# Score products of a sparse-attention branch: keys stacked as high and low rows, low queries beside rows of zeros

## The chip, the core and the metric

The kernel runs on one core of a Trainium2 chip. Its engines are named as in the profile: PE (TensorE, matrix products; PEld is its loading of stationary operands), DVE (VectorE), ACT (ScalarE), POOL (GpSimd) and SP (SyncE, which issues most DMAs). The metric is the device time of one execution in microseconds (us); the number given for a kernel is the median of its runs.

## What is computed

One layer of a hybrid decoder with 256 tokens and a width of 2048. One wide projection of x feeds four branches (spatial gating, a gated recurrence, sparse attention, attention into memory tokens); each branch is gated, projected to 2048 columns and merged, and an output projection with a residual and a LayerNorm closes the layer. The change lies in the sparse attention. With 256 tokens its "selected" and "window" branches both see every key up to the query, so both are ordinary causal attention with their own keys and values; four key/value heads serve 16 query heads of 64 columns:

```python
s = jnp.einsum('bhgqd,bhqnkd->bhgqnk', q_b, ks).astype(f32).reshape(...) + bias
p = masked_softmax(s, mask)
o_s = jnp.einsum('bhgqnk,bhqnkd->bhgqd', p.astype(vs.dtype), vs)
...
s_w = jnp.einsum('bhgqd,bhkd->bhgqk', q_b, kw).astype(f32) + bias_w
p_w = masked_softmax(s_w, mask_w)
o_w = jnp.einsum('bhgqk,bhkd->bhgqd', p_w.astype(vw.dtype), vw)
...
o = g[0] * o_c + g[1] * o_s + g[2] * o_w
```

## The kernel before

Everything is float32. A large product is made from operands that are split in two parts of the type fp32r: the high part is a cast (ACT), the low part is what the cast left over (DVE). Of the four part products three are taken: high by high, high by low, low by high. The weights (some 240 MB) come from HBM in chunks of 1024 words on each of 128 partitions. `prepare` (lines 161 to 184) loads a chunk, casts it (`whi`) and subtracts (`wlo`), two chunks ahead of its use; three buffers hold the high parts and three the low parts. Two loops use the chunks: `gemm_b` (lines 191 to 209) keeps the weights in PE and moves 256 tokens, high and low side by side, past them (lines 202 and 203, tile `mmb`); `gemm_a` (lines 218 to 232) keeps the tokens and moves 512 weight columns past them, three products for each of two token tiles (lines 214 to 216, tile `mma`).

All other work is cut into items, closures that are put into a list by `start_side(items, chunks)`. After each chunk of a large product `pump` runs as many items as `len(items) / chunks` says, so the number of items and the number of chunks set at which chunk an item comes. What an item does on ACT and DVE is put behind the newest split of weights. The order of the instructions on each engine is then fixed ahead of the run by a scheduler that works with its own estimate of times. Engines take their instructions strictly in this order.

The two lists of items that matter here:

- The first runs beside the value projections of the two branches (lines 499 to 517, tile `vs`, 12 chunks of up to 840 words). Its items are four times `make_flat` (lines 418 to 428: four DVE additions into `flat`, a cast and a subtraction into `fhl`) and four times `split_k` (lines 489 to 497). `split_k` makes, for a pair of key heads, the high part of each head's 64 key rows on both halves of the partitions (`khd`, two casts for each head) and the low part in place (`klo`, one subtraction for each head).
- The second runs beside the merge of the memory branch and the projection after it, 48 chunks (lines 657 to 665). For each pair of query heads j, `split_q` (lines 592 to 599) puts the high part of a head's queries on its own 64 partitions and the low part on the other 64; `nsa_probs` (lines 601 to 629) makes the scores of one head, 512 keys for the second 128 queries (`s1`) and 256 for the first 128 (`s0`), and the softmax; `nsa_trans` transposes the probabilities (lines 635 to 637, tile `pt`); `nsa_values` (lines 642 to 654, tile `po`) multiplies them with the values, in products with 64 output rows (line 651).

A head's scores take four products: line 608 has 128 rows (high and low queries, against the high keys on both halves), line 609 has 64 rows (high queries against the low keys), and lines 611 and 612 do the same for the first 128 queries. The profile names the score tiles `s`.

Of the kernel before, what the change touches and what calls it, by code (L numbers as in the profile page):

```python
# [14 lines left out]
P = 128  # L15
# [3 lines left out]
CH = 1024            # float32 words of one weight chunk on a partition (512 KB in all)  # L19
# [3 lines left out]
NWV = 280            # columns of the chunks that hold values and gate logits  # L23

# [1 line left out]
BUCKET_COUNTS = [1] * 16 + [5, 6, 8, 11, 13, 18, 22, 29, 38, 50, 40]  # L26

# [7 lines left out]
NB = 16 * P // CH          # chunks of one 128-column product  # L35
NA = 16 * 512 // CH        # chunks of one 512-column product over 2048 rows
NH = 8 * 512 // CH         # the same over 1024 rows
# [12 lines left out]
def tile_hybrid_layer(ctx: ExitStack, tc: tile.TileContext, wb, wv, xT, memT, x, params, cmpp, biasp, consts,  # L50
# [19 lines left out]
    # ================= helpers =================  # L70
# [27 lines left out]
    def after(later, earlier):  # L98
        """both on one engine: later is issued after earlier."""
        tc.add_manual_dep(later.ins, earlier.ins.name,  # L100
                          mybir.DependencyInfo(mybir.DependencyClass.NoSync, mybir.DependencyReason.DATA),
                          reason="order on the engine")

# [1 line left out]
    # An item's work on VectorE and ScalarE is issued after the newest split of weights before it.  # L105
# [85 lines left out]
    def gemm_b(src, d, evac=None):  # L191
        """[128 columns, 256 tokens] into d: the weights stay, both parts of the tokens move past them at once."""
        ps = psum(mm, "mmb")
        nk = CH // P
        for c in range(NB):
            hi, lo = next_chunk()
            for kk in range(nk):
                k = c * nk + kk
                xs = src[k // 8][:, k % 8]
                wh = hi[:, kk * P:(kk + 1) * P]  # L200
                wl = lo[:, kk * P:(kk + 1) * P]
                nc.tensor.matmul(ps, wh, xs, start=(k == 0), stop=False)  # L202
                nc.tensor.matmul(ps[:, 256:512], wl, xs[:, 0:256], start=False, stop=(k == 15))  # L203
            if c == NB - 1:
                vec.tensor_copy(d, ps[:, 0:256])
                vec.tensor_add(d, d, ps[:, 256:512])
                if evac:
                    evac()
            pump()
# [8 lines left out]
    def gemm_a(src, nkt, evac):  # L218
        """[128 tokens, 512 columns] for both token tiles: the tokens stay, the weights move."""
# [14 lines left out]
    def rstd(y, v, name, w=1, follow=None):  # L234
        """y = 1 / sqrt(v + eps), with one Newton step."""
# [15 lines left out]
    # ================= memory values and keys =================  # L251
    def load_hl(src, hl, i, part=None):
        """k tiles 2 i and 2 i + 1 of the tokens, split."""
# [61 lines left out]
    # ================= memory attention =================  # L315
# [11 lines left out]
    def o_store(hl, j, o_ps, g):  # L327
        """o * silu gate, split into the two parts of the operand."""
        o = prob("oraw", 256)
        vec.tensor_mul(o, o_ps, g)  # L330
        split(hl[:, j, 0:256], hl[:, j, 256:512], o)
# [4 lines left out]
    def mm_3(ps, w, c0, xs, first, last):  # L336
        """columns c0.. of w (high parts in front, low parts 256 behind) with 256 moving columns."""
# [53 lines left out]
    # ================= projections of the sparse attention =================  # L391
    # in the order k_c, v_c, k_s, k_w; two key/value head pairs each
# [19 lines left out]
    # its two parts side by side: one product of both with the high part of w1, one of the high part with the low one  # L412
# [73 lines left out]
    khd = [big("kh0", "khd0", F32R, (P, 2, 512)), big("kh1", "khd1", F32R, (P, 2, 512))]  # L486
    klo = big("va1", "klo", F32R, (P, 2, 512))

    def split_k(pr, br):
        src = kbr[br][pr]  # L490
        cs = slice(br * 256, (br + 1) * 256)
        for half in range(2):
            hs = slice(half * 64, half * 64 + 64)
            os = slice(64 - half * 64, 128 - half * 64)
            act.copy(khd[half][hs, pr, cs], src[hs])
            act.copy(khd[half][os, pr, cs], src[hs])
            vec.tensor_sub(klo[hs, pr, cs], src[hs], khd[half][hs, pr, cs].bitcast(F32))

    start_side([lambda b=b, pr=pr: make_flat(b, pr) for b in range(2) for pr in range(2)] +
               [lambda pr=pr, br=br: split_k(pr, br) for br in range(2) for pr in range(2)], 11)  # L500

# [90 lines left out]
    def split_q(j):  # L592
        q = scr("qs", 512, F32R).rearrange("p (h t) -> p h t", h=2)
        for half in range(2):
# [3 lines left out]
            vec.tensor_sub(q[os, half], qT[j][hs], q[hs, half].bitcast(F32))  # L598
        qs[j] = q

    def nsa_probs(j, half):
        hs = slice(half * 64, half * 64 + 64)
        hd = 2 * j + half
        q = qs[j]
        kh, kl = khd[half][:, j // 4], klo[:, j // 4]
        s1 = psum(scp, "s1")
        s0 = psum(scp, "s0")
        nc.tensor.matmul(s1, q[:, half, P:256], kh, start=True, stop=False)
        nc.tensor.matmul(s1, q[hs, half, P:256], kl[hs], start=False, stop=True)  # L609
        k0 = lambda a: a.rearrange("p (b k) -> p b k", b=2)[:, :, 0:P]  # L610
        nc.tensor.matmul(s0[:, 0:256], q[:, half, 0:P], k0(kh), start=True, stop=False)
        nc.tensor.matmul(s0[:, 0:256], q[hs, half, 0:P], k0(kl[hs]), start=False, stop=True)
# [54 lines left out]
    # ================= merge of the branches =================  # L667
# [26 lines left out]
    # ================= convolution and RG-LRU =================  # L694
    # softplus(-lambda) = max(-lambda, 0) + log1p(exp(-|lambda|)), log1p(u) = 2 atanh(u / (2 + u))
# [54 lines left out]
    def lru_tanh():  # L750
        # t = tanh(-log_a / 2) = (1 - a) / (1 + a): 1 - a = 2 t / (1 + t), 1 - a^2 = 4 t / (1 + t)^2
# [20 lines left out]
    def lru_scan(c):  # L772
        t, s = ri[:, c, 0:256], ri[:, c, 256:512]
        w, v = lqs[c][:, 0:256], lqs[c][:, 256:512]
        # w = 1 / (s (1 + t)); one Newton step of the root: 2 sqrt(t) = s + t / s
# [21 lines left out]
    # ================= chunked spatial gating =================  # L797
# [111 lines left out]
    # ================= output projection, residual, norm =================  # L909
# [60 lines left out]
def _chunks_b(w, c0, n):  # L970
    """n column tiles of 128: [128 rows of a k tile, k tiles, 128]."""
# [9 lines left out]
def _chunks_a(w, c0, width=512):  # L981
    """one column tile of 512: [128 rows of a k tile, k tiles, 512]."""
# [94 lines left out]
```

## Time and profile before

| what | value |
|---|---|
| time, median of 3 runs | 1308.05 us (1307.18 to 1309.77) |
| the profiled execution: span from first to last instruction | 1305.8 us |
| PE busy | 1279.2 us (98%) |
| DVE busy | 836.7 us (64%) |
| ACT busy | 654.0 us (50%) |
| POOL busy | 122.7 us (9%) |
| mean granted clock of PE | 0.993 of full speed |
| chain that ended last | PE 89%, POOL 5%, DVE 3%, DMA 2%, ACT 1% |

The span is the profiled execution's own time between its first and its last instruction; the measured time of a run also holds what lies around it, here 1308.05 - 1305.8 = 2.25 us by the median. Busy time of PE is modelled: products overlap, so one of them shows as some 390 ns in the list of instructions even where the next ends 230 ns later. What a product costs in a gapless stretch is its step in the chain of waits, the time from the end of the one before to its own end.

### The profile page before, as it was taken

How to read it: one execution, taken by the hardware profiler on the slowest of the kernel's cores; microseconds unless marked ns; L12 is line 12 of the kernel's file. 1: busy time of each engine (PE TensorE's matmuls, PEld its weight loads, DVE VectorE, ACT ScalarE, POOL GpSimd, SP SyncE). 2: the span in 40 equal slices, each digit the busy share in tenths (PEclk: the TensorE clock that was granted, in tenths of full speed). 3: DMA queues.
4: the chain of work that ended last, by engine and by line, in shares of the span. 5: the costliest groups of instructions: out<-in, count | busy, mean ns of one | idle time of the engine just before them, and what ended most of it. 6: DMA issues, size and time to landing. Idle time of an engine off the chain costs nothing.

```text
span 1305.8 us, 17559 instructions
## 1 busy us (share of the span) xinstructions
PE 1279.2 (98%) x6588; PEld 1070.8 (82%) x6588; DVE 836.7 (64%) x1306; ACT 654.0 (50%) x921; POOL 122.7 (9%) x128
## 2 busy tenths in 40 slices
PE   8999999999999999999999899999999999999996
PEld 6888898988887777778888688888888888888886
DVE  6666665686557566677667896455556555555556
ACT  6544564375448656655763454444444444444442
POOL 0000000000000000002289800000000000000001
PEclk9999999999999999999999899999999999999998
DMA  9766659567565444446555566666666666668662
GB/s 314 239 191 181 179 150 206 159 214 237 180 190 162 146 138 137 146 130 193 167 172 178 154 209 201 188 192 194 195 199 192 195 193 195 184 187 320 191 214 79
DMA packets 74699, 244.57 MB, mean 187 GB/s; under 512 B 8663, under 2 KB 14967, under 8 KB 74103
## 3 DMA queue, kind: packets, MB, share of 16 engines
q1 hardware_dynamic: 70752, 235.53, 59.3%
q10 hardware_dynamic: 3863, 7.93, 2.6%
q8 instruction: 51, 0.84, 0.3%
q14 instruction: 33, 0.27, 0.1%
HBM read 240.94 MB, written 2.49 MB: 186 GB/s over the span
## 4 chain that ended last, share of the span: by engine, by line
PE 89%; POOL 5%; DVE 3%; DMA 2%; ACT 1%; issue 1%; SPq 0%; ACTq 0%
PE mmb L202 19%; PE mma L215 17%; PE mma L214 17%; PE mma L216 17%; PE mmb L203 10%; DMA raw<-in_wb 2%; DVE wlo L114 1%; PE po L651 1%; POOL ri L764 1%; POOL lq L766 1%; DVE flat L114 1%; PE mmd L216 1%; PE mmd L215 1%; PE mmd L214 1%; PE s L609 1%
## 5 line engine op out<-in xcount | busy, mean ns | idle before, releaser
L114 DVE TENSOR_TENSOR wlo<-raw,whi 128x1024 fp32r<-128x1024 f32 (+2 forms) x429 | 529.2, 1235 | 384.3 <-ACT whi L114 377.2
L114 ACT CAST whi<-raw 128x1024 fp32r<-128x1024 f32 (+2 forms) x429 | 446.7, 1042 | 514.1 <-PE mma L216 277.6
L202 PE MATMUL mmb<-xhl,whi 128*128 128x512 f32 x1152 | 411.4, 400 | 5.9 <-ACT whi L114 5.9
L203 PE MATMUL mmb<-xhl,wlo 128*128 128x256 f32 x1152 | 325.6, 283 | 2.5 <-DVE wlo L114 2.5
L202 PEld LDWEIGHTS mmb<-xhl,whi 128*128 128x128 f32 x1152 | 217.7, 189 | 57.5 <-ACT whi L114 6.9
L215 PE MATMUL mma<-wlo,xhl 128*128 128x512 f32 x576 | 226.4, 393 | 0.0
L203 PEld LDWEIGHTS mmb<-xhl,wlo 128*128 128x128 f32 x1152 | 219.0, 190 | 7.3 <-DVE wlo L114 5.0
L216 PE MATMUL mma<-whi,xhl 128*128 128x512 f32 x576 | 224.8, 390 | 0.0
L214 PE MATMUL mma<-whi,xhl 128*128 128x512 f32 x576 | 206.9, 392 | 0.0
L215 PEld LDWEIGHTS mma<-wlo,xhl 128*128 128x128 f32 x576 | 108.2, 188 | 21.9 <-issue 0.6
L216 PEld LDWEIGHTS mma<-whi,xhl 128*128 128x128 f32 x576 | 108.2, 188 | 21.9
L214 PEld LDWEIGHTS mma<-whi,xhl 128*128 128x128 f32 x576 | 107.7, 188 | 22.4 <-issue 0.4
L736 POOL CAST lwhl<-lw 128x256 fp32r<-128x256 f32 x8 | 5.9, 744 | 622.9 <-DVE oc L114 605.2
L202 PE MATMUL mmb<-memhl,whi 128*128 128x512 f32 x128 | 45.3, 399 | 0.0
L114 ACT ACT_TABLE_LOAD x31 | 39.8, 1283 | 3.8 <-issue 1.6
L215 PE MATMUL mma<-wlo,mT 128*128 128x512 f32 x96 | 37.5, 390 | 0.0
L216 PE MATMUL mma<-whi,mT 128*128 128x512 f32 x96 | 37.4, 390 | 0.0
L203 PE MATMUL mmb<-memhl,wlo 128*128 128x256 f32 x128 | 35.9, 281 | 0.0
L214 PE MATMUL mma<-whi,mT 128*128 128x512 f32 x96 | 33.6, 390 | 0.0
L114 ACT ACTIVATE p<-p,mn 128x256 f32<-128x256 f32 x64 | 28.6, 448 | 7.3 <-DVE mn L114 5.4
L875 POOL TENSOR_TENSOR ws<-ws,smask 128x128 f32<-128x128 f32 x8 | 6.7, 840 | 269.9 <-DMA ws<-in_sguw 269.9
L202 PEld LDWEIGHTS mmb<-memhl,whi 128*128 128x128 f32 x128 | 24.1, 188 | 6.0
(301 smaller groups left out, 1677.7 us busy)
## 6 DMA issues: line engine op xcount, KB each, us to landing
raw<-in_wb SPq DMA_DIRECT2D x423, 512.0 KB, 4.2
raw<-in_wv SPq DMA_DIRECT2D x10, 420.0 KB, 3.3
traw<-in_xT SPq DMA_DIRECT2D x8, 256.0 KB, 5.8
bt<-bdr ACTq DMA_DIRECT2D x8, 256.0 KB, 11.2
z<-in_x ACTq DMA_DIRECT2D x1, 2048.0 KB, 9.2
out<-z SPq DMA_DIRECT2D x8, 256.0 KB, 2.3
traw<-in_memT SPq DMA_DIRECT2D x7, 256.0 KB, 6.0
lw<-in_lruw SPq DMA_DIRECT2D x8, 128.0 KB, 4.4
```

The lines of the kernel that those rows point to most:

```text
L114: ins = getattr(getattr(nc, self.name), op)(*a, **k)
L202: nc.tensor.matmul(ps, wh, xs, start=(k == 0), stop=False)
L203: nc.tensor.matmul(ps[:, 256:512], wl, xs[:, 0:256], start=False, stop=(k == 15))
L214: nc.tensor.matmul(ps, xh, wh, start=first, stop=False)
L215: nc.tensor.matmul(ps, xh, wl, start=False, stop=False)
L216: nc.tensor.matmul(ps, xl, wh, start=False, stop=last)
L609: nc.tensor.matmul(s1, q[hs, half, P:256], kl[hs], start=False, stop=True)
L651: nc.tensor.matmul(po[hs, kt * P:256], vsw[:, kt, br, kvh * 64:(kvh + 1) * 64], pT[:, 256:384] if kt else pT[:, 0:256], start=False, stop= ...
L736: nc.gpsimd.tensor_copy(lws[c][:, 0:256], lw)
L764: nc.gpsimd.tensor_scalar(s, s, 2.0 ** -55, 1e-30, op0=ALU.mult, op1=ALU.max)
L766: nc.gpsimd.tensor_mul(w, v, s)
L875: nc.gpsimd.tensor_mul(ws[:, 0:P], ws[:, 0:P], smask)
```

## The change

The key tiles `khd` become `khl`: a head's high rows stay on its own half, and its low rows stand on the other half. The tile `klo` goes; its place takes `qlz`, which holds the low queries of a head on its own half and zeros on the other, for two pairs of heads in turn. The tile of high queries `q` now has the high part on both halves. Each of the four products of a head has 128 rows: high queries (twice) against high and low keys, and low queries over zeros against the same. The products keep their number and their numbers of columns. A new item `zero_rows` with two memsets makes the list of 8 items a list of 9, over the same 11 chunks. All else in the two files differs only in comments.

```diff
-    khd = [big("kh0", "khd0", F32R, (P, 2, 512)), big("kh1", "khd1", F32R, (P, 2, 512))]
-    klo = big("va1", "klo", F32R, (P, 2, 512))
+    khl = [big("kh0", "khl0", F32R, (P, 2, 512)), big("kh1", "khl1", F32R, (P, 2, 512))]
+
+    qlz = big("va1", "qlz", F32R, (P, 2, 2, 256))
...
-            act.copy(khd[half][hs, pr, cs], src[hs])
-            act.copy(khd[half][os, pr, cs], src[hs])
-            vec.tensor_sub(klo[hs, pr, cs], src[hs], khd[half][hs, pr, cs].bitcast(F32))
+            act.copy(khl[half][hs, pr, cs], src[hs])
+            vec.tensor_sub(khl[half][os, pr, cs], src[hs], khl[half][hs, pr, cs].bitcast(F32))
+
+    def zero_rows():
+        for half in range(2):
+            vec.memset(qlz[64 - half * 64:128 - half * 64, :, half].bitcast(F32), 0.0)
 
     start_side([lambda b=b, pr=pr: make_flat(b, pr) for b in range(2) for pr in range(2)] +
-               [lambda pr=pr, br=br: split_k(pr, br) for br in range(2) for pr in range(2)], 11)
+               [lambda pr=pr, br=br: split_k(pr, br) for br in range(2) for pr in range(2)] + [zero_rows], 11)
...
             act.copy(q[hs, half], qT[j][hs])
-            vec.tensor_sub(q[os, half], qT[j][hs], q[hs, half].bitcast(F32))
+            act.copy(q[os, half], qT[j][hs])
+            vec.tensor_sub(qlz[hs, j % 2, half], qT[j][hs], q[hs, half].bitcast(F32))
...
-        kh, kl = khd[half][:, j // 4], klo[:, j // 4]
+        k1 = khl[half][:, j // 4]
+        k0 = k1.rearrange("p (b k) -> p b k", b=2)[:, :, 0:P]
         s1 = psum(scp, "s1")
         s0 = psum(scp, "s0")
-        nc.tensor.matmul(s1, q[:, half, P:256], kh, start=True, stop=False)
-        nc.tensor.matmul(s1, q[hs, half, P:256], kl[hs], start=False, stop=True)
-        k0 = lambda a: a.rearrange("p (b k) -> p b k", b=2)[:, :, 0:P]
-        nc.tensor.matmul(s0[:, 0:256], q[:, half, 0:P], k0(kh), start=True, stop=False)
-        nc.tensor.matmul(s0[:, 0:256], q[hs, half, 0:P], k0(kl[hs]), start=False, stop=True)
+
+        nc.tensor.matmul(s1, q[:, half, P:256], k1, start=True, stop=False)
+        nc.tensor.matmul(s1, qlz[:, j % 2, half, P:256], k1, start=False, stop=True)
+        nc.tensor.matmul(s0[:, 0:256], q[:, half, 0:P], k0, start=True, stop=False)
+        nc.tensor.matmul(s0[:, 0:256], qlz[:, j % 2, half, 0:P], k0, start=False, stop=True)
```

The scheduler's order changes with it. Three places are shown; the names are tiles, with a number where several tiles share a name, and the score products stand on lines 614 to 617 of the changed kernel, the value products on line 656.

PE, one head's scores in the merge of the memory branch, before:

```order
L216 MATMUL mma_3847<-whi,om 128x512
L608 MATMUL s_3896<-khd_2328,qs 128x512
L609 MATMUL s_3896<-klo,qs 128x512
L611 MATMUL s_3897<-khd_2328,qs 128x256
L612 MATMUL s_3897<-klo,qs 128x256
L214 MATMUL mma_3846<-whi,om 128x512
```

and in the changed kernel:

```order
L216 MATMUL mma_3843<-whi,om 128x512
L614 MATMUL s_3892<-khl_2328,qs 128x512
L615 MATMUL s_3892<-khl_2328,qlz 128x512
L616 MATMUL s_3893<-khl_2328,qs 128x256
L617 MATMUL s_3893<-khl_2328,qlz 128x256
L214 MATMUL mma_3842<-whi,om 128x512
```

The four products stand in the same place; only their operands differ.

DVE, beside the value projections, from the last chunk of the first branch on, before (`raw` numbers are weight chunks, `gate` the logits behind the first branch):

```order
L114 TENSOR_TENSOR wlo<-raw_2417,whi 128x280
L114 TENSOR_TENSOR fhl<-flat,fhl 128x16x30
L114 TENSOR_TENSOR wlo<-raw_2441,whi 128x840
L114 TENSOR_TENSOR flat<-kv_2023,cpar 64x16x15 x4
L114 TENSOR_TENSOR wlo<-raw_2471,whi 128x840
L114 TENSOR_TENSOR flat<-kv_2071,cpar 64x16x15 x4
L114 TENSOR_TENSOR gate<-vs_2331,gb 128x24
L114 TENSOR_TENSOR gate<-vs_2332,gb 128x24
L114 TENSOR_TENSOR wlo<-raw_2495,whi 128x840
```

and in the changed kernel:

```order
L114 TENSOR_TENSOR wlo<-raw_2417,whi 128x280
L114 TENSOR_TENSOR flat<-kv_2023,cpar 64x16x15 x4
L114 TENSOR_TENSOR fhl<-flat,fhl 128x16x30
L114 TENSOR_TENSOR wlo<-raw_2447,whi 128x840
L114 TENSOR_TENSOR flat<-kv_2071,cpar 64x16x15 x4
L114 TENSOR_TENSOR fhl<-flat,fhl 128x16x30
L114 TENSOR_TENSOR wlo<-raw_2477,whi 128x840
L114 TENSOR_TENSOR gate<-vs_2331,gb 128x24
L114 TENSOR_TENSOR gate<-vs_2332,gb 128x24
L114 TENSOR_TENSOR wlo<-raw_2495,whi 128x840
```

The third and the fourth group of `flat` additions each stand one chunk earlier, ahead of a `wlo` that they stood behind.

PE, the value products of the second pair of heads, before:

```order
L644 MATMUL po<-pcT_3754,vbd 128x256
L651 MATMUL po<-pT,vsw 64x128 x2
L651 MATMUL po<-pT,vsw 64x256 x2
L651 MATMUL po<-pT,vsw 64x128 x2
L651 MATMUL po<-pT,vsw 64x256 x2
L215 MATMUL mma_4321<-wlo,om 128x512
```

and in the changed kernel:

```order
L649 MATMUL po<-pcT_3748,vbd 128x256
L656 MATMUL po<-pT,vsw 64x128 x2
L656 MATMUL po<-pT,vsw 64x256 x2
L656 MATMUL po<-pT,vsw 64x128
L216 MATMUL mma_4321<-whi,om 128x512
L214 MATMUL mma_4320<-whi,om 128x512
L215 MATMUL mma_4320<-wlo,om 128x512
L216 MATMUL mma_4320<-whi,om 128x512
L214 MATMUL mma_4321<-whi,om 128x512
L656 MATMUL po<-pT,vsw 64x128
L656 MATMUL po<-pT,vsw 64x256 x2
L215 MATMUL mma_4321<-wlo,om 128x512
```

Here one run of eight products with 64 output rows became two runs with five large products between them. Over all eight pairs there were 12 such runs before and there are 13 now.

## Rows read from the trace of the kernel before

**Rows 1.** First lines of the page: span, then busy us, share, instructions.

```profile
span 1305.8 us, 17559 instructions
PE 1279.2 (98%) x6588; PEld 1070.8 (82%) x6588; DVE 836.7 (64%) x1306; ACT 654.0 (50%) x921; POOL 122.7 (9%) x128
```

**Rows 2.** Stretch: us, busy PE, PEld, DVE, ACT, POOL, PE clock, DMA.

```profile
395.00:610.00 215.00, 215.00 (x1078) 166.16 (x1077) 147.64 (x434) 135.77 (x274) 4.37 (x6) 1.00 0.49 147
```

**Rows 3.** Chain of waits, one head's scores: start us, us, what.

```profile
461.76 0.23 PE s L608
461.99 0.42 PE s L609
462.41 0.32 PE s L611
462.73 0.31 PE s L612
463.04 0.43 PE mma L214
```

**Rows 4.** Chain of waits, transposes behind another head's scores.

```profile
427.88 0.26 PE pt L635
428.14 0.11 PE pt L636
```

**Rows 5.** Chain of waits, the one L611 that stands behind transposes.

```profile
529.09 0.12 PE s L611
```

**Rows 6.** Chain of waits, a 256-column product near the end.

```profile
1272.40 0.12 PE mmd L214
```

**Rows 7.** Stationary loads of line 608: ns min/median/max, first and last us, form.

```profile
L608 PEld LDWEIGHTS s<-khd,qs x16: 186/187/189, 402.0 to 579.8; 128*128 128x128 f32 x16
```

**Rows 8.** DVE in order of time: start us, us, instruction, count.

```profile
261.08 0.65 DVE L114 TENSOR_TENSOR fhl<-flat,fhl 128x480 fp32r<-128x480 f32 x1
261.65 1.02 DVE L114 TENSOR_TENSOR wlo<-raw,whi 128x840 fp32r<-128x840 f32 x1
262.60 2.34 DVE L114 TENSOR_TENSOR flat<-kv,cpar 64x240 f32<-64x240 f32 x4
264.97 1.03 DVE L114 TENSOR_TENSOR wlo<-raw,whi 128x840 fp32r<-128x840 f32 x1
265.92 2.34 DVE L114 TENSOR_TENSOR flat<-kv,cpar 64x240 f32<-64x240 f32 x4
```

**Rows 9.** PE there, first low product of three chunks; in brackets the wait.

```profile
266.06 0.40 PE L215 MATMUL vs<-wlo,xhl 128*128 128x280 f32 x1 [0.75 <-DVE wlo L114]
...
274.40 0.29 PE L215 MATMUL vs<-wlo,xhl 128*128 128x280 f32 x1
...
276.71 0.29 PE L215 MATMUL vs<-wlo,xhl 128*128 128x280 f32 x1
```

**Rows 10.** Chain of waits, value products of one pair in two runs.

```profile
478.33 1.01 PE po L651 x10
...
480.24 0.79 PE po L651 x5
```

**Rows 11.** Chain of waits, value products of another pair, unbroken.

```profile
502.36 1.45 PE po L651 x16
```

**Rows 12.** Groups by line and shape, ACT: count, busy us, mean ns, idle.

```profile
L114 ACT CAST qs<-q 64x256 fp32r<-64x256 f32 x16 | 6.4, 402 | 0.2
```

**Rows 13.** Groups by line and shape, DVE: memsets of 512 words.

```profile
L114 DVE MEMSET pc<- 128x512 f32 x2 | 1.0, 485 | 0.1
```

**Rows 14.** DVE, the low part of one chunk in the score stage.

```profile
411.62 1.23 DVE L114 TENSOR_TENSOR wlo<-raw,whi 128x1024 fp32r<-128x1024 f32 x1
```

**Rows 15.** PE, its first product with that low part.

```profile
415.06 0.40 PE L215 MATMUL mma<-wlo,om 128*128 128x512 f32 x1
```

**Rows 16.** ACT, held until POOL releases a buffer.

```profile
722.10 1.04 ACT L114 CAST whi<-raw 128x1024 fp32r<-128x1024 f32 x1 [9.82 <-POOL ri L783]
```

**Rows 17.** PE behind that cast.

```profile
723.20 0.80 PE L202 MATMUL mmb<-xhl,whi 128*128 128x512 f32 x1 [5.04 <-ACT whi L114]
```

More of the change, by code (lines that the diff above doesn't have):

```diff
@@ L597, in split_q @@
             act.copy(q[hs, half], qT[j][hs])
-            vec.tensor_sub(q[os, half], qT[j][hs], q[hs, half].bitcast(F32))
+            act.copy(q[os, half], qT[j][hs])
+            vec.tensor_sub(qlz[hs, j % 2, half], qT[j][hs], q[hs, half].bitcast(F32))
         qs[j] = q
     def nsa_probs(j, half):
-        hs = slice(half * 64, half * 64 + 64)
         hd = 2 * j + half
         q = qs[j]
-        kh, kl = khd[half][:, j // 4], klo[:, j // 4]
+        k1 = khl[half][:, j // 4]
+        k0 = k1.rearrange("p (b k) -> p b k", b=2)[:, :, 0:P]
         s1 = psum(scp, "s1")
         s0 = psum(scp, "s0")
-        nc.tensor.matmul(s1, q[:, half, P:256], kh, start=True, stop=False)
-        nc.tensor.matmul(s1, q[hs, half, P:256], kl[hs], start=False, stop=True)
-        k0 = lambda a: a.rearrange("p (b k) -> p b k", b=2)[:, :, 0:P]
-        nc.tensor.matmul(s0[:, 0:256], q[:, half, 0:P], k0(kh), start=True, stop=False)
-        nc.tensor.matmul(s0[:, 0:256], q[hs, half, 0:P], k0(kl[hs]), start=False, stop=True)
+        nc.tensor.matmul(s1, q[:, half, P:256], k1, start=True, stop=False)
+        nc.tensor.matmul(s1, qlz[:, j % 2, half, P:256], k1, start=False, stop=True)
+        nc.tensor.matmul(s0[:, 0:256], q[:, half, 0:P], k0, start=True, stop=False)
+        nc.tensor.matmul(s0[:, 0:256], qlz[:, j % 2, half, 0:P], k0, start=False, stop=True)
         for br in range(2):
```

## Prediction

> **What bounds the kernel now.** I read the head of the page first. PE is busy for 1279.2 of 1305.8 us [rows 1], so a gain must come out of PE's own sequence, and a loss shows as a wait of PE. Then I looked at the stage that holds the score products, the stretch from 395 to 610 us: PE is busy in all of its 215.00 us at a clock of 1.00, that is 2.4 GHz, while DVE works for 147.64 and ACT for 135.77 us [rows 2]. PE waits for nobody there, so every step that leaves PE's chain in this stretch moves the end by its own length, as long as ACT and DVE keep up.
>
> Next came the chain of waits at one head's scores, where the reader compares steps of equal column counts [rows 3]. Line 608, with 128 rows and 512 columns, takes 0.23 us. Line 609, also 512 columns but 64 rows, takes 0.42. Lines 611 and 612 have 256 columns each and take 0.32 and 0.31, and the large product behind them, which takes 0.23 elsewhere, takes 0.43. A transpose behind the scores takes 0.26 where the next takes 0.11 [rows 4]. So some 0.2 us is added at each passage from 128 rows to 64 and from 64 to 128. It belongs to the passage and not to the line: the one line 611 that follows transposes with 128 rows takes 0.12 [rows 5]. The size agrees with a stationary load of 187 ns that is no longer hidden [rows 7].
>
> **The change: the score products.** Nothing is removed from PE but these passages. The new steps are taken from products with 128 rows: 0.23 for 512 columns [rows 3] and 0.12 for 256 columns, each with a stationary operand of its own [rows 5, 6]. A head followed by a large product costs 0.42 + 0.32 + 0.31 + 0.43 = 1.48 us with its follower now, and 0.23 + 0.12 + 0.12 + 0.23 = 0.70 then: 0.78 saved. A head followed by a transpose goes from 1.31 (0.26 in place of 0.43) to 0.58: 0.73 saved. The chain shows 7 heads of the first kind, 8 of the second, and one that is broken by transposes and loses four passages as well (0.74). The sum is 7 x 0.78 + 8 x 0.73 + 0.74 = 12.0 us. The value products with 64 output rows keep their own passages.
>
> The row just read also weighs a rule. Line 608 uses all 128 rows, follows a product that does so too, and still takes 0.23 us with a load of 187 ns [rows 3, 7]: that load lay beside the product before it. The Trainium skill says otherwise (TensorE: Matmul & The Clock Gate, The mechanism): a load of weights overlaps products in flight only when their row groups differ. By that rule the new products would hide no load at all, and the gain would be none; the trace speaks against it here. This is rival 1 below.
>
> **The change: the list of nine items.** Nine items in place of eight over the same 11 chunks come at chunks 2, 3, 4, 5, 7 and on in place of 2, 3, 5, 6, 7, 9 and on. The third and fourth group of `flat` additions thereby stand ahead of a `wlo` that they stood behind, and DVE is what PE waits for just there [rows 9]. Worked forward in DVE's order with the steps of before: the first `fhl` starts at 261.08, and the four additions take 2.34 [rows 8], so they end at 263.42, `fhl` (261.65 - 261.08 = 0.57) at 263.99, and `wlo` 1.03 later at 265.02 against 262.67. From its next start at 264.94 (a step is 262.60 - 261.65 = 0.95) four additions, `fhl` and `wlo` follow: 264.94 + 2.34 + 0.57 + 1.03 = 268.88, against 266.00 now. PE's first low product of this chunk then starts at 268.94 in place of 266.06, 2.9 us late. Part of that is made good, since the following `wlo` has now no `flat` group before it: it ends some 1.2 us later, at 270.0, before PE needs it. PE goes on at its pace of 276.71 - 274.40 = 2.31 us a chunk [rows 9]. Four chunks on it stands at 268.94 + 4 x 2.31 = 278.18, against 276.71: 1.5 us late. The bounds are 0 (the weights of these chunks come late for another reason in both kernels) and 2.9 (nothing is made good). I take 1.5, the value of the worked order.
>
> The two memsets write 512 words on 64 partitions each. A memset of 512 words on 128 partitions takes 485 ns [rows 13], so they add 1.0 us to DVE behind the last of the eight old items, where by the count above PE's need lies over 1 us later. I count 0; without that cover it is 1.0.
>
> **The change: value products.** The new order has 13 runs of products with 64 output rows in place of 12. A pair in two runs costs 1.01 + 0.79 us [rows 10] plus one more large product at 0.43 in place of 0.23; an unbroken pair costs 1.45 [rows 11]. The difference is 0.55 us, lost. Bounds are 0 and 1.1.
>
> **The change: casts.** Eight casts of 64 rows leave ACT at 264 to 277 us, where ACT waits anyway: nothing gained. In the score stage 16 casts of 0.402 us are added [rows 12], 6.4 us on an ACT with 79 us to spare [rows 2]. Behind each pair of them stands the `whi` of a coming chunk, and behind that its `wlo` and PE. The tightest chunk that I found has its low part at 411.62 + 1.23 = 412.85 [rows 14] and is first used at 415.06 [rows 15]: 2.2 us of cover against 0.8 us of casts and at most two heads' gain (1.5 us). It is just enough, and elsewhere the cover is 2.5 us or more. I count 0; bounds 0 and 6.4. DVE's subtractions only change their target. No DMA is added; on SP one load for the recurrence changes places with one weight chunk in this stage, where PE has no wait to lengthen.
>
> **A wait further on.** At 712 to 722 us ACT is held for 9.82 us by a DMA that it has to issue into a buffer that POOL still uses [rows 16], and PE waits 5.04 us for the cast behind it [rows 17]. The change swaps some of POOL's instructions in this recurrence, with the same instructions ahead of the one that frees the buffer. PE, ACT and POOL all arrive earlier together, so I count 0; bounds are -5.0 (the wait goes) and +5.0 (it doubles).
>
> **The sum.** -12.0 + 1.5 + 0.55 = -10.0 us. Against the profiled execution: 1305.8 - 10.0 = 1295.8 us of span, and with the 2.25 us around it, which the change doesn't touch, 1298.1 us, which is also 10.0 below the median of 1308.05.
>
> **Rivals.**
> 1. *The loads stay in the open.* If a load can't be hidden between two products that use the same rows, then the first score product, the three behind it and the follower each pay 0.2 us: five passages a head in place of four, 16 x 0.2 = 3.2 us more than now, with 1.5 and 0.55 lost besides: 1313.3 us, slower. It decides at the step of the second product of a head: 0.4 us rather than 0.23. For it speaks only that these operands come from new tiles; against it that 0.23 and 0.12 are paid everywhere else with 128 rows [rows 3, 6].
> 2. *ACT comes late.* The added casts push `whi` behind PE's need, and PE waits for all 6.4 us: 1304.5 us. For it speaks the cover of 2.2 us in the first heads, against it that ACT stands idle for a third of the stage [rows 2].
> 3. *The wait behind POOL changes size.* POOL's new order frees the buffer earlier or later and moves PE's 5.04 us by its whole length: 1293.1 or 1303.1 us.
>
> **How the numbers follow.** The forecast has a chance of 0.74, with 1294.5 to 1302 as its own range from the bounds of 1.5, 0.55 and part of the last term. Rival 1 has 0.04, rival 2 0.10, rival 3 0.12 with both signs. The range of 1293.0 to 1303.2 us takes in the forecast and rival 3, 0.86 in all. A difference of 0.2% (2.6 us) is about what the measurement can tell from no change. Faster by more holds the forecast, rival 3 and most of rival 2: 0.92. Within 0.2%: 0.04. Slower: 0.04.
>
> **What would show it.** In the chain of the changed kernel lines 614 to 617 should step by 0.23, 0.23, 0.12 and 0.12 us and the follower by 0.23 or 0.11; a 0.4 there is rival 1. PE's waits for `wlo` at 262 to 271 us should grow from under 2 us to about 3.2. There should be no wait of PE for `whi` or `wlo` between 395 and 600 us; several are rival 2. The wait behind POOL near 712 us (ten earlier than now) should stay near 5 us. A time above 1305 us would mean that the passages were not what costs 0.2 us, or that their gain is given back at a place that I hold for covered.

## The result and the profile after

The changed kernel takes 1298.51 us (median), against 1308.05 before: a ratio of 0.9924, with an interval of 0.9911 to 0.9936. The forecast was 1298.1. The profiled execution of that timing was disturbed and took 3658 us, so the profile shown here is from a second timing of the same kernel (1298.62 us, ratio 0.9921, interval 0.9904 to 0.9938; its profiled execution 1298.26 us).

The head of its page, in the columns of [rows 1]:

```profile
span 1296.1 us, 17572 instructions
PE 1268.3 (98%) x6588; PEld 1071.4 (83%) x6588; DVE 836.9 (65%) x1308; ACT 655.8 (51%) x929; POOL 124.8 (10%) x128
```

PE executes as many instructions as before and is busy 10.9 us less; the span is 9.7 us shorter. So the gain lies in PE's own sequence, and 1.2 us of it went into further waits. The stretch of the score products, as in [rows 2]:

```profile
395.00:610.00 215.00, 215.00 (x1136) 175.35 (x1135) 155.67 (x447) 148.87 (x303) 8.60 (x10) 1.00 0.52 158
```

PE is still busy throughout at a clock of 1.00 (2.4 GHz), and gets 1136 instructions done where it did 1078. ACT now works for 148.87 us of the 215.

A head's scores in the chain of waits (start us, us, what), which answers to [rows 3, 4]; lines 614 to 617 are the four products, 640 is the transpose behind them:

```profile
426.35 0.23 PE s L614
426.58 0.23 PE s L615
426.80 0.12 PE s L616
426.92 0.12 PE s L617
427.04 0.11 PE pt L640
```

The stationary loads of the second of these lines, grouped as in [rows 7]:

```profile
L615 PEld LDWEIGHTS s<-khl,qlz x16: 187/188/192, 403.3 to 572.1; 128*128 128x128 f32 x16
```

The steps are 0.23, 0.23, 0.12 and 0.12 us, and the transpose takes 0.11 in place of 0.26: no product pays for a passage. The loads of 187 to 192 ns lie beside products that use the same 128 rows. Here the rule that stood behind rival 1 (the Trainium skill, TensorE: Matmul & The Clock Gate, The mechanism: a load overlaps products in flight only where the row groups differ) is contradicted by the trace. The same section also lets a load into a background weight buffer go ahead of products in flight, and that would fit.

PE's waits by releaser (total us, times, longest):

```profile
PE mmb L202 <- ACT whi L114: 7.7, 2, 6.6
PE vs L215 <- DVE wlo L114: 3.5, 2, 2.3
```

The second line is the list of nine items; the first is the wait behind POOL. Both in order of time (start us, us, instruction, in brackets the wait and its releaser): PE at the values, as in [rows 9], then ACT and PE behind POOL, as in [rows 16, 17]:

```profile
264.69 0.40 PE L215 MATMUL vs<-wlo,xhl 128*128 128x280 f32 x1 [2.25 <-DVE wlo L114]
...
268.56 0.40 PE L215 MATMUL vs<-wlo,xhl 128*128 128x280 f32 x1 [1.27 <-DVE wlo L114]
```

```profile
712.57 1.99 ACT L114 CAST whi<-raw 128x1024 fp32r<-128x1024 f32 x2 [11.42 <-POOL ri L788]
```

```profile
713.67 0.79 PE L202 MATMUL mmb<-xhl,whi 128*128 128x512 f32 x1 [6.64 <-ACT whi L114]
```

Four landmarks cut the span into pieces: the first and last high product of the values (`vs`, line 216), ACT's last Gelu of `vact`, and the first product of the last merge (`mT`, line 214). The end of the scores lies between the second and the third. For before and after in that order (min/median/max ns, first to last start):

```profile
L216 PE MATMUL vs<-whi,xhl x64: 287/291/298, 250.3 to 277.1; 128*128 128x280 f32 x64
L114 ACT ACTIVATE vact<-mma x4: 590/597/600, 636.2 to 664.0; 128x512 f32<-128x512 f32 x4
L214 PE MATMUL mma<-whi,mT x96: 389/389/476, 1204.2 to 1271.1; 128*128 128x512 f32 x96
```

```profile
L216 PE MATMUL vs<-whi,xhl x64: 287/291/293, 249.9 to 278.3; 128*128 128x280 f32 x64
L114 ACT ACTIVATE vact<-mma x4: 592/595/599, 626.4 to 653.6; 128x512 f32<-128x512 f32 x4
L214 PE MATMUL mma<-whi,mT x96: 389/389/476, 1194.5 to 1261.4; 128*128 128x512 f32 x96
```

| stretch | before | after | difference | forecast |
|---|---|---|---|---|
| start to first `vs` | 250.3 | 249.9 | -0.4 | 0 |
| first to last `vs` | 26.8 | 28.4 | +1.6 | +1.5 |
| last `vs` to last `vact` | 386.9 | 375.3 | -11.6 | -12.0 + 0.55 |
| last `vact` to first `mT` | 540.2 | 540.9 | +0.7 | 0 (-5 to +5) |
| first `mT` to the end | 101.6 | 101.6 | 0.0 | 0 |

### The profile page after: what moved, and what is told of

It is laid out like the page before. It is cut to its first block, busy times and chain, and to the rows that moved or that the text cites. A ratio compares the mean times of both kernels' runs of the same rounds, so it can differ in the third digit from the quotient of the medians.

```text
span 3656.6 us, 17572 instructions
## 1 busy us (share of the span) xinstructions
PE 3643.2 (100%) x6588; PEld 2353.9 (64%) x6588; DVE 831.4 (23%) x1308; ACT 662.8 (18%) x929; POOL 99.1 (3%) x128
## 4 chain that ended last, share of the span: by engine, by line
PE 100%; DVE 0%; ACT 0%; ACTq 0%; issue 0%
PE mmb L202 26%; PE mma L215 17%; PE mma L214 17%; PE mma L216 17%; PE mmb L203 13%; PE po L656 1%; PE vs L214 1%; PE vs L216 1%; PE vs L215 1%; PE mmd L215 1%; PE mmd L216 1%; PE mmd L214 1%; PE hps L442 0%; PE hps L441 0%; PE pt L641 0%; PE s L615 0%
## 5 line engine op out<-in xcount | busy, mean ns | idle before, releaser
L202 PE MATMUL mmb<-xhl,whi 128*128 128x512 f32 x1152 | 1123.0, 978 | 0.0
L203 PE MATMUL mmb<-xhl,wlo 128*128 128x256 f32 x1152 | 707.3, 614 | 0.0
L202 PEld LDWEIGHTS mmb<-xhl,whi 128*128 128x128 f32 x1152 | 452.4, 393 | 344.9 <-issue 342.0
L215 PE MATMUL mma<-wlo,xhl 128*128 128x512 f32 x576 | 494.7, 859 | 0.0
L216 PE MATMUL mma<-whi,xhl 128*128 128x512 f32 x576 | 490.5, 852 | 0.0
L203 PEld LDWEIGHTS mmb<-xhl,wlo 128*128 128x128 f32 x1152 | 470.0, 408 | 25.8 <-issue 7.1
L214 PE MATMUL mma<-whi,xhl 128*128 128x512 f32 x576 | 465.4, 854 | 0.0
L214 PEld LDWEIGHTS mma<-whi,xhl 128*128 128x128 f32 x576 | 206.8, 360 | 142.4 <-issue 140.6
L215 PEld LDWEIGHTS mma<-wlo,xhl 128*128 128x128 f32 x576 | 207.1, 360 | 141.0 <-issue 139.3
L216 PEld LDWEIGHTS mma<-whi,xhl 128*128 128x128 f32 x576 | 207.6, 360 | 140.0 <-issue 139.6
L202 PE MATMUL mmb<-memhl,whi 128*128 128x512 f32 x128 | 140.6, 1098 | 0.0
L216 PE MATMUL mma<-whi,memhl 128*128 128x512 f32 x64 | 69.6, 1097 | 0.0
L214 PE MATMUL mma<-whi,memhl 128*128 128x512 f32 x64 | 66.0, 1101 | 0.0
```

Source lines behind the costliest of these rows:

```text
L214: nc.tensor.matmul(ps, xh, wh, start=first, stop=False)
L215: nc.tensor.matmul(ps, xh, wl, start=False, stop=False)
L216: nc.tensor.matmul(ps, xl, wh, start=False, stop=last)
```

## The experiments

Every kernel was timed beside the kernel before on the same chip, in four sets; its time there was 1309.12 us (e1 to e4), 1309.29 (e5 to e8), 1308.52 (e9 to e11) and 1309.37 (e12). Ratios are against that. "The score stretch" below is the third line of the table.

**e1: the changed kernel again.**

> The changed kernel once more, for an undisturbed trace. By the prediction's steps: lines 614 to 617 step by 0.23, 0.23, 0.12, 0.12 us, the follower by 0.23 or 0.11; PE waits about 3.2 us for wlo beside the value projections (1.7 before); no wait between 395 and 600 us; the wait behind POOL near 5 us. Time 1298.5 us. If instead ACT came late or the gain came from elsewhere, waits appear in the score stage, or the steps of 615 and 617 stay at 0.4 and 0.3 us and the time was won at another place.

1298.62 us, and all steps as above. It is the base for what follows.

**e2: eight items again, the memsets inside the last of them.**

```diff
     def split_k(pr, br):
+        if pr and br:
+            zero_rows()
...
-               [... for br in range(2) for pr in range(2)] + [zero_rows], 11)
+               [... for br in range(2) for pr in range(2)], 11)
```

> The changed kernel with the two memsets inside the last of the eight old items, so that the list has 8 items over 11 chunks as before. If the nine-item list costs what was worked out, PE's waits for wlo fall from 3.2 to 1.7 us and the time from 1298.5 to 1297.0 us. If those chunks are late for another reason, or the cost is made good later, the time stays at 1298.5 us.

1297.17 us, ratio 0.9905 (0.9888 to 0.9922), 1.45 us under e1. The waits at the low products of `vs` are back at the size of before:

```profile
PE vs L215 <- DVE wlo L114: 1.7, 2, 0.9
```

**e3: the kernel before with an empty ninth item.**

```diff
-               [... for br in range(2) for pr in range(2)], 11)
+               [... for br in range(2) for pr in range(2)] + [lambda: None], 11)
```

> The kernel before with an empty ninth item in the first list and nothing else. If the pace alone costs 1.5 us, the time goes from 1308.1 to 1309.6 us, with PE's waits for wlo at about 3.2 us. If the pace costs nothing: 1308.1 us.

1310.69 us, ratio 1.0017 (1.0005 to 1.0028): 1.57 us slower, and the same wait as in the changed kernel:

```profile
269.42 0.40 PE L215 MATMUL vs<-wlo,xhl 128*128 128x280 f32 x1 [2.26 <-DVE wlo L114]
```

The differences in time of e2 and e3 are near the spread of the runs, and the intervals of e1 and e2 overlap. The stage itself is clearer: from the first to the last `vs` it takes 26.8 us before and 26.9 in e2 (eight items), 28.4 after and 28.3 in e3 (nine items). So the number of items costs 1.5 us, and the memsets themselves cost nothing where they stand beside other work.

**e4: the low products cut back to the 64 rows of their half.** Operands, copies and the order of all instructions stay those of the changed kernel.

```diff
-        nc.tensor.matmul(s1, qlz[:, j % 2, half, P:256], k1, start=False, stop=True)
+        nc.tensor.matmul(s1, qlz[hs, j % 2, half, P:256], k1[hs], start=False, stop=True)
...
-        nc.tensor.matmul(s0[:, 0:256], qlz[:, j % 2, half, 0:P], k0, start=False, stop=True)
+        nc.tensor.matmul(s0[:, 0:256], qlz[hs, j % 2, half, 0:P], k0[hs], start=False, stop=True)
```

> The changed kernel with its two low-query products cut back to the 64 rows that are not zero; keys, queries, items and the order of all instructions stay as in the changed kernel. If the passages between 128 and 64 rows are the whole gain, all four come back at every head: 16 heads, 12.0 us in all, 1310.5 us. If the gain came from the new layout or the new order, the time stays at 1298.5 us.

1313.06 us, ratio 1.0022 (1.0008 to 1.0037). The whole gain is gone. The steps of [rows 3] are back:

```profile
469.65 0.23 PE s L615
469.88 0.42 PE s L616
470.30 0.32 PE s L617
470.61 0.31 PE s L618
470.92 0.43 PE mma L215
```

The score stretch takes 387.1 us, 11.8 more than after. PE's order in this kernel has 62 passages at the score products (one head's two low products stand side by side), so one costs 11.8 / 62 = 0.19 us. The median is 2.5 us over what was expected; in the profiled run some 4 us of that lie ahead of the first `vs`, where the kernels are alike, so it says nothing of the change.

**e5: only the fourth product on 64 rows.**

```diff
-        nc.tensor.matmul(s0[:, 0:256], qlz[:, j % 2, half, 0:P], k0, start=False, stop=True)
+        nc.tensor.matmul(s0[:, 0:256], qlz[hs, j % 2, half, 0:P], k0[hs], start=False, stop=True)
```

> The changed kernel, with only the fourth score product of a head (s0 with the low queries, 256 columns) back on the 64 rows of its half; the order of all instructions stays. Passages cost (a change between 128 and 64 rows costs 0.2 us, 0.15 ahead of a transpose): a head has two passages in place of none, at line 618 (0.32 in place of 0.12) and at its follower (0.43 or 0.26 in place of 0.23 or 0.11), so 0.37 a head and 16 x 0.37 = 5.9 us: half of what the low products of both s1 and s0 on 64 rows cost, 1298.6 + 5.9 = 1304.5 us. The steps ahead stay at 0.23, 0.23, 0.12. If the gain of the change came from elsewhere (the copies of q, the keys' new places, the order of the list), nothing moves: 1298.6 us.

1304.35 us, ratio 0.9971 (0.9960 to 0.9982), half of the gain as expected. Two passages a head are left, at the 64-row product and behind it:

```profile
468.34 0.23 PE s L615
468.57 0.23 PE s L616
468.79 0.11 PE s L617
468.91 0.31 PE s L618
469.22 0.43 PE mma L215
```

The score stretch is 5.7 us longer than after, 0.18 a passage.

**e6: both low products on 64 rows, one behind the other.**

```diff
+        nc.tensor.matmul(s0[:, 0:256], q[:, half, 0:P], k0, start=True, stop=False)
-        nc.tensor.matmul(s1, qlz[:, j % 2, half, P:256], k1, start=False, stop=True)
+        nc.tensor.matmul(s1, qlz[hs, j % 2, half, P:256], k1[hs], start=False, stop=True)
-        nc.tensor.matmul(s0[:, 0:256], q[:, half, 0:P], k0, start=True, stop=False)
-        nc.tensor.matmul(s0[:, 0:256], qlz[:, j % 2, half, 0:P], k0, start=False, stop=True)
+        nc.tensor.matmul(s0[:, 0:256], qlz[hs, j % 2, half, 0:P], k0[hs], start=False, stop=True)
```

> The changed kernel with the score products in another order: both products of the high queries with 128 rows first (0.23 and 0.12), then both of the low queries on 64 rows, one behind the other. Two theories of the 0.2 us. It belongs to the passage between 128 and 64 rows: the first low product takes 0.42, the second, 64 rows behind 64 rows, takes 0.12, the follower 0.43 or 0.26; two passages a head, 5.9 us, 1304.5 us as with one low product on 64 rows. It belongs to each product with 64 rows, whose load cannot lie beside another product: the second takes 0.32 too, 16 x 0.2 = 3.2 us more, 1307.7 us.

1306.21 us, ratio 0.9981 (0.9970 to 0.9992): between the two expectations, so the time alone doesn't decide. The steps do:

```profile
477.48 0.23 PE s L615
477.71 0.11 PE s L616
477.82 0.43 PE s L617
478.25 0.12 PE s L618
478.37 0.26 PE pt L641
```

The second 64-row product (line 618) takes 0.12 us. It isn't the 64 rows that cost, but the passage to them and back. The stationary loads of the same head show what is paid (start us, us, in brackets how long the loading stood idle):

```profile
477.75 0.18 PEld L617 LDWEIGHTS s<-khl,qlz 64*128 64x128 f32 x1 [0.24 <-issue]
477.86 0.19 PEld L618 LDWEIGHTS s<-khl,qlz 64*128 64x128 f32 x1
478.30 0.14 PEld L641 LDWEIGHTS pt<-ident,p 128*128 128x128 f32 x1 [0.25 <-issue]
```

At the passage to 64 rows the load starts at 477.75, shortly before the product ahead of it ends (477.82), and its 0.18 us stand in the open. The next load, with the same 64 rows, starts at 477.86 and lies beside product 617, which ends at 478.25. At the passage back the load of the transpose takes 0.14 us and again starts late, and the transpose is dearer by 0.15.

The score stretch is 6.7 us longer than after, 1.0 more than in e5. At the last two heads the scheduler did not keep the sequence of the edit; there product 616, with 128 rows, stands between the two low ones:

```profile
580.18 0.32 PE s L616
580.50 0.31 PE s L618
```

So these heads have four passages, and there are 14 x 2 + 2 x 4 = 36 in all, where e5 has 32: 6.7 / 36 = 0.19 us each. The four more explain 0.75 of the 1.0 us.

**e7: the added cast three times.** The copy of a query half onto the other partition half is repeated.

```diff
             act.copy(q[os, half], qT[j][hs])
+            act.copy(q[os, half], qT[j][hs])
+            act.copy(q[os, half], qT[j][hs])
```

> The changed kernel, in which the new cast of a query half onto the other partition half is done three times in place of once: 32 further ACT casts of 402 ns, 12.9 us of work on ACT in the stretch of the scores, where ACT is busy for 136 of 215 us. If ACT's work there is covered, as the forecast says: the casts cost nothing, and the sequence of the value products, which has 14 runs in place of 13 in this order, costs 0.4 to 0.55 us: 1299.1 us, with no wait of PE for whi or wlo between 395 and 600 us. If what stands on ACT there is paid by PE (the rival with ACT late): up to 12.9 us more, 1311 us, with several waits for whi.

1302.34 us, ratio 0.9951 (0.9934 to 0.9968): 3.7 over e1, more than the forecast and far from 12.9. The score stretch is 378.0 us, 2.7 longer than after. Of that 0.4 to 0.55 is one more run of value products, and 1.3 are waits of PE, first of all this one:

```profile
538.62 0.47 PE L616 MATMUL s<-khl,qs 128*128 128x512 f32 x1 [1.12 <-DVE mn L114]
```

About 1 us is left unexplained. With 12.9 us of additional work on ACT, PE loses between 1.3 and 2.3 us, so the 6.4 us that the change adds, after which PE waits nowhere in this stretch, are covered, but there is not much cover left.

**e8: zero-padded values.** e2, with 64 columns of zeros beside each half's values, so that the value products have 128 columns too. GpSimd clears 512 words.

```diff
-    vsw = big("va0", "vsw", F32, (P, 2, 2, 256))
+    vsw = big("va0", "vsw", F32, (P, 2, 2, 2, 192))
+    nc.gpsimd.memset(vsw[:, :, :, :, 64:128], 0.0)
...
-                    nc.tensor.matmul(po[hs, kt * P:256], vsw[:, kt, br, kvh * 64:(kvh + 1) * 64],
+                    nc.tensor.matmul(po[:, kt * P:256], vsw[:, kt, br, j // 4, half * 64:half * 64 + P],
```

> The kernel that clears the zero rows inside the last old item (1297.2 us), with the same idea applied to the value products: each half's 64 columns of values stand beside 64 columns of zeros, so that the products write 128 rows of po and the stationary operand has 128 columns throughout; GpSimd clears 512 words a partition once. If the passage costs the same for 64 columns as for 64 rows: the 13 runs of value products lose a dearer first product (0.43 to 0.23 at its second or first product) and a dearer follower (0.43 to 0.23, or 0.26 to 0.11), 13 x 0.38 = 5.0 us, 1292.2 us, and the steps behind a run read 0.23 or 0.11. If the loss of a run belongs to the products (f32 operands, two passes each) and not to the passage: 1297.2 us, no change.

1302.39 us, ratio 0.9954 (0.9941 to 0.9967): 5.2 slower than e2, where 5.0 faster was expected. The passages did go. In the chain of waits a pair of e8, and below it one of e2:

```profile
435.55 2.62 PE po L658 x16
438.17 0.11 PE pt L644
```

```profile
434.13 1.45 PE po L658 x16
435.58 0.26 PE pt L642
```

The transpose behind the run takes 0.11 us in place of 0.26. But the 16 products take 2.62 us in place of 1.45. In e2 the chain has 3 unbroken pairs at 1.45 and 5 at 1.01 + 0.79, 13.35 us in all; in e8 it is 8 x 2.62 = 20.96. That is 7.6 lost, against 2.5 gained at 13 followers: 5.1. The score stretch is 4.6 us longer than in e2 (380.3 against 375.7), with seven products fewer in it (2028 against 2035).

**e9: value products in another sequence, in 8 unbroken runs.** e2, with those first that need the latest probabilities.

```diff
-        for br in range(2):
+        for br in (1, 0):
             for kt in (1, 0):
-                for half in range(2):
+                for half in (1, 0):
```

> The kernel that clears the zero rows inside the last old item (1297.2 us), with the eight value products of a pair in another sequence: those come first that need the probabilities transposed last, so that the order keeps all 8 pairs unbroken, 8 runs of value products in place of 13. By the forecast's price (a pair in two runs costs 1.01 + 0.79 and one dearer follower, 0.55 us more than an unbroken one at 1.45): 5 x 0.55 = 2.75 us less, 1294.4 us. If the run's price is paid anyway, because PE now waits for the last transposed probabilities: 1297.2 us and waits of PE for pT.

1307.8 us, ratio 0.9995 (0.9986 to 1.0004): by the ratios some 11 us slower than e2. The score stretch takes 370.5 us, down from 375.7, but that is not the gain it seems. The scheduler made another order of much else, and PE starts 1999 products in this stretch where e2 has 2035. Of the 36 that now stand behind it 24 are gate products of the recurrence (0.12 us each in the chain of waits) and 12 are products with weights (0.23 and 0.12), an estimated 5.0 us of the 5.2. PE also waits 2.1 us in the stretch, and nowhere in that of e2. So five runs fewer are worth an estimated 2.3 us, near the 2.75 expected.

With its gate products the recurrence on POOL comes late. POOL's first step on `xc` for e2, and below it for e9 (first and last start); its last step starts 9 us later (742.7 and 752.1 us):

```profile
L755 POOL TENSOR_TENSOR xc<-xc,ri x8: 736/742/1673, 604.3 to 647.8; 128x256 f32<-128x256 f32 x8
```

```profile
L755 POOL TENSOR_TENSOR xc<-xc,ri x8: 737/740/744, 624.4 to 664.6; 128x256 f32<-128x256 f32 x8
```

DVE waits for POOL there, the low parts stand behind DVE's scans, and PE waits for the low parts ten times, 12.6 us in all where e2 has three such waits with 1.6:

```profile
PE mmb L203 <- DVE wlo L114: 12.6, 10, 2.3
```

The profiled execution is the fastest of e9's runs; its span is 5.8 us over that of e2. Where the rest of the 11 us lies these traces do not show, and that the late recurrence is the cause is read from the waits, not tested.

**e10: e9, with the half as the outer loop**, four products of one half and then four of the other.

```diff
-        for br in (1, 0):
+        for half in (1, 0):
-            for kt in (1, 0):
+            for br in (1, 0):
-                for half in (1, 0):
+                for kt in (1, 0):
```

> The kernel with the unbroken value products (1294.4 us expected), with the half as the outer loop: the four products of one 64-column half first, then the four of the other, in place of half by half in turn. Of two theories of why 16 products take 1.45 us with 64 columns and 2.62 us with 128: two products on different 64-column halves of PE run side by side, then nothing can run side by side here, a pair takes some 2.6 us, and the kernel 8 x 1.17 = 9.4 us more, 1303.8 us. Or a stationary operand of 64 columns loads and steps faster by itself (its load is 132 to 137 ns in place of 187): 1.45 us a pair as before, 1294.4 us.

1312.83 us, ratio 1.0036 (1.0024 to 1.0049), 5.0 slower than e9 on the same chip. A pair now takes 2.15 us:

```profile
435.79 2.15 PE po L658 x16
```

8 x (2.15 - 1.45) = 5.6 us, and the score stretch is 5.4 us longer than in e9, with as many products in it. Neither expected number came. The sequence alone, with the same products and the same loads of 132 to 138 ns, moves a pair from 1.45 to 2.15. The single starts in the traces show why. In e2 the 16 passes of a pair (two for each of its eight products) start two and two, 7 ns apart (434.064 and 434.071, 434.224 and 434.231 us, and so on): two rows of eight run side by side, each in steps of 0.11 us for 128 columns and 0.215 for 256. In e8 the passes start one by one, in the same steps. In e10 the first row starts at 435.72 us and the second at 436.42, and only the middle of the run is shared: 0.71 + 1.45 = 2.16 us. So products of the two 64-column halves do run side by side; why the second row starts where it does in e10 is left open.

**e11 and e12: the rows of the norm in tiles of their own.** On e9 (e11) and on e2 (e12), `lg` and `lb` go into the two tiles that held the keys.

```diff
+    lnt = [big(f"kh{n}", f"lnt{n}", F32, (P, 2, 512)) for n in range(2)]
...
-        lg = scr("lg")
+        lg, lb = lnt[n][:, 0], lnt[n][:, 1]
         nc.scalar.dma_start(lg, ...)
-        lb = scr("lb")
         nc.scalar.dma_start(lb, ...)
```

> The kernel with the unbroken value products (1294.4 us expected), with the scale and bias rows of the first token norm (lg, lb) in the two tiles of the keys, which are free after the last scores, in place of scratch tiles that POOL releases one by one. Their four loads, issued by ACT, then wait for nothing that POOL does. If ACT stands for 11.4 us and PE for 6.6 us near 712 us because the load of lg is held in ACT's queue until POOL frees a scratch tile: both waits go, 1294.4 - 6.6 = 1287.8 us. If PE waits there since POOL's work itself is late for what follows: no change, 1294.4 us, with a wait of PE of 5 us or more behind another step of POOL.

1308.2 us against 1307.8 for e9: no change. It could not tell the theories apart, since the wait of 6.6 us is not in e9 to begin with (its longest wait for `whi` is 1.7 us).

> The kernel that clears the zero rows inside the last old item (1297.2 us, PE waits of 6.6 us behind POOL near 712 us), with the scale and bias rows of the first token norm (lg, lb) in the two tiles of the keys, which are free after the last scores, in place of scratch tiles that POOL releases one by one. Here the order of all other work stays as it is, but for three products and one wlo near 480 us. If ACT stands for 11.4 us and PE for 6.6 us because the load of lg is held in ACT's queue until POOL frees a scratch tile: both waits go, 1297.2 - 6.6 = 1290.6 us. If POOL's work itself is late for what comes behind it: 1297.2 us, with a wait of 5 us or more behind another step of POOL.

1295.38 us, ratio 0.9901 (0.9885 to 0.9917), the fastest of all, 14.0 under the kernel before on its chip; e2 was 12.0 under. By the intervals the two can't be told apart. In the profiled run the wait of ACT and that of PE are both gone, so the load held in ACT's queue was their cause. All that PE still waits for `whi` at this line:

```profile
PE mmb L202 <- ACT whi L114: 0.8, 1, 0.8
```

Windows of e2 and then of e12 (columns as in [rows 2]):

```profile
670.00:720.00 50.00, 42.87 (x229) 36.45 (x228) 38.57 (x41) 18.17 (x22) 49.60 (x52) 0.91 0.54 166
720.00:740.00 20.00, 20.00 (x114) 17.51 (x113) 19.64 (x21) 8.68 (x11) 16.10 (x15) 0.97 0.59 186
```

```profile
670.00:720.00 50.00, 50.00 (x285) 43.26 (x284) 47.24 (x50) 23.13 (x28) 49.68 (x47) 1.00 0.62 190
720.00:740.00 20.00, 17.78 (x95) 14.78 (x94) 16.00 (x17) 7.02 (x9) 19.61 (x22) 0.96 0.47 143
```

Between 670 and 720 us PE starts 56 products more than in e2, at a clock of 1.00 in place of 0.91. Then DVE waits for POOL, and part of it is given back; from the last `vact` to the first `mT` 537.6 us are left of 541.6, 4.0 in place of the 6.6 expected:

```profile
740.88 0.69 DVE L114 TENSOR_TENSOR_SCAN xb<-ri,xc 128x256 f32<-128x256 f32 x1 [3.07 <-POOL xc L788]
```

## Why the prediction was right

*PE bounds the stage, and a step that leaves its chain moves the end by its length.* Right: the score stretch lost 11.6 us and the span 9.7. All that came behind the scores moved ahead with it. That the time came within 0.4 us of the forecast is in part luck: 0.7 us lost behind the scores, which were not counted, stand against 0.4 us at the start, where the kernels are alike.

*The 0.2 us belongs to the passage between 128 and 64 rows.* Shown. Putting the low products back on 64 rows in an unchanged order brings 11.8 us back (e4), putting back one of two brings 5.7 (e5), and a 64-row product behind another takes 0.12 us (e6). The prediction took the size for that of a stationary load that is no longer hidden; the loads in e6 bear it out, 0.18 us in the open at a product that is dearer by 0.2 and 0.14 at a transpose that is dearer by 0.15. The Trainium skill (TensorEngine Tiling (Array Packing), Key Properties) says that a change of the tiling mode drains TensorE, which agrees with loads that start only as the product ahead ends; it gives no price, and here the price is 0.18 to 0.19 us on average (e4, e5, e6).

*The size of that term, 12.0 us.* By e4's price the 64 passages of the kernel before cost 64 x 0.19 = 12.2 us.

*The nine items, +1.5.* Right: +1.6 in the `vs` stage, where e2 and e3 show that it goes and comes with the ninth item. The waits grew from under 2 to 3.5 us, where 3.2 was forecast.

*One more run of value products, +0.55.* It has no experiment of its own; e9, with five runs fewer, gives an estimated 0.46 a run. -11.6 + 12.2 leaves 0.6 for it, and the same price explains that e4's score stretch is 0.2 longer than that of before, with two passages fewer (0.55 - 0.38). That is worked out, not measured alone.

*Casts, 0.* Right, with less to spare than was said: three times the added work shows in PE's time (e7).

*The wait behind POOL, 0.* Mis-sized: not all three engines came earlier by the same amount. PE begins to wait 11.1 us earlier than before (707.03 and 718.16 us), but POOL has freed the buffer, so that ACT can issue the load, only 9.5 us earlier (712.10 and 721.62), so the wait grew from 5.0 to 6.6 us. POOL's steps stand in another order there; e2 and e4, with the order of after, show 6.6 as well, and e3, with the order of before, 5.0. That the order is the cause was not tested by itself. Since the stretch around it only grew by 0.7 us, most of that was made good before the last merge. The text had its cause right: e12 takes the load out of ACT's queue, and the wait goes.

Rival 1 would have shown 0.4 at the second product of a head; it took 0.23. Rival 2 needed waits between 395 and 600 us; there are none. Rival 3 came about on the slower side, at a third of its size.

## What to carry to other kernels

Where products of different tile shapes (128 rows, 64 rows, 64 columns) stand in turn on a busy PE, count the passages: at some 0.2 us each, rows of zeros can be cheaper than a small product. Count first what the small shape gives: 64-column products of two halves in turn took less time here than in any other way tried, since they ran side by side, and padding them lost more than the passages had cost. And compare the whole order that a scheduler makes, and the number of products in a stretch before its length is read as a gain: in e9 an edit of the value products alone put 36 other products behind the score stage, the recurrence on POOL started 20 us later, and the gain of the change was gone.

## What was not expected of the hardware

- 16 value products with 64 columns, halves in turn, take 1.45 us; with one half after the other 2.15; with 128 columns 2.62. In the first case two passes run at a time.
- A wait of PE can cost more than its length. During the 6.64 us in which PE does nothing the granted clock falls to 0.50, that is to 1.2 GHz, and PE's work behind the wait runs at that clock until after 720 us. From 715 to 720 us PE gets 16 products done, where it does 29 in the next 5 us (after; columns as in [rows 2]). The difference, 13 products or some 2.2 us, adds to the wait. In e12, without the wait, the clock is 1.00 from 670 to 720 us.

```profile
715.00:720.00 5.00, 5.00 (x16) 4.33 (x17) 4.97 (x7) 2.22 (x3) 4.92 (x6) 0.50 0.67 193
720.00:725.00 5.00, 5.00 (x29) 4.30 (x28) 4.79 (x6) 2.42 (x3) 2.18 (x3) 0.95 0.65 190
```
